# One PSUM bank per purpose, evictions queued at once, and dense work cut into quanta, in a fused encoder block

## The chip, the cores and the metric

The kernel runs on all 8 cores of one Trainium2 chip. Each core takes half of one sequence of the batch of four; there is no exchange between cores. The metric is device time in microseconds (us) of the slowest core. Most runs of one kernel agree within 0.3%, but some fall into a slow state; only fast runs are compared.

## The reference, cut to what matters

One encoder layer: normalization, one wide input projection, latent attention with 16 heads, a gated width-3 convolution, a merge of both, an output projection, and a last gated embedding.

```python
h   = rmsnorm(x);  z = h @ w_in                    # latents, rope key, gates, conv B/C/x, merge gates
q, kv from the latents (w_uq, w_ukv), per-head QK-norm, rope, softmax over 2048 keys
y_attn = (attn * silu(gate_a)) @ w_branch_attn
y_conv = (B * conv3(C * xin) * silu(gate_c)) @ w_branch_conv
x = x + (sigmoid(m_a) * y_attn + sigmoid(m_c) * y_conv) @ w_out
x = x + sigmoid(rmsnorm(x) @ w_ple_gate) * (p @ w_ple_proj)
```

Per core there are 1024 queries and 2048 keys. Three kinds of TensorE work meet in the middle of the kernel: the attention itself (16 heads x 16 steps of 128 keys), the small "pieces" that prepare the next head (Q, K, V from the latents, sums of squares) and close the last one, and "dense" groups of 16 matmuls each, for the attention gates (32 groups) and the eight channel blocks of the convolution (10 groups each).

## The kernel before: the parts that matter

PSUM, which all matmuls of the kernel write (`ps<-` in the traces), is used as eight banks. Scores take four (two steps in flight), the output two. Banks 6 and 7, `F`, are left for pieces and dense groups. Whoever needs a bank takes the one that is free and least recently used; the eviction (the operations that read the bank) is put on a list and queued later.

```python
F = [banks[6], banks[7]]
def grab(keep=False):                       # a bank for a piece, or (keep) for a dense group
    free = [i for i in (0, 1) if held[i] is None]
    i = min(free, key=lambda j: lastuse[j])
    ...
    flush()                                 # queues the evictions put off so far
    if keep: held[i] = True
    return i, F[i]

def proj16(tile_, rhs, n):                  # a dense group
    i, bk = grab(keep=True)
    for kc in range(16):
        mm(bk.ap[:, 0:n], tv[:, kc, :], rhs(kc), kc == 0, kc == 15, ...)
        yield n / 512.0                     # fill(n) asks for n of these at a time
    release(i)
    return bk

def qrope(i):                               # one of the pieces
    _, bk = grab()
    ...                                     # eight matmuls
    def ev(): ...                           # ACT square and VectorE product out of the bank
    deferred.append(ev)

for h in range(NH):                         # the attention; g = 16 * h + kt
    ...
    for kt in range(16):
        emit_S(g + 1)                       # scores of the next step into PSUM
        emit_exp(g + 1)                     # ACT: exp of them, 128x1024
        flush()                             # only now the evictions of the step before
        for fn in now:                      # pieces of the next head
            fn(); fill(budget / (len(now) + 1))
        fill(budget / (len(now) + 1))       # dense matmuls: gates and convolutions, some 5 a step
        emit_PV(g)
        emit_acc(g)                         # VectorE: running sum of the exponentials
```

ACT and VectorE work through their queues in order, as two pieces of trace below show: under run 4, ACT's copy of K starts at 612.01 us, behind an exp (611.00) before which ACT had been idle for 2.83 us; under run 7, VectorE's t1b starts at 669.78, behind Qn (668.27, after 0.33 us of waiting for ACT) and Qr (669.06). Semaphores are derived from the buffers that each operation reads and writes: a matmul that overwrites a bank waits for the operations that read it (here, in the attention, 41.8 us in 28 waits for fq alone).

Of the kernel before, what the change touches and what calls it, by code (L numbers as in the profile page):

```python
# [18 lines left out]
NH = 16  # L19
# [154 lines left out]
def build_nc():  # L174
# [20 lines left out]
    with ExitStack() as es:  # L195
# [61 lines left out]
        def mm(bank_ap, lhsT, rhs, start, stop, reads, writes, skip=False):  # L257
            if skip:
                return P.op("pe", lambda h: h.matmul(bank_ap, lhsT=lhsT, rhs=rhs, start=start, stop=stop, skip_group_check=True), reads=reads, writes=writes)  # L259
            return P.op("pe", lambda h: h.matmul(bank_ap, lhsT=lhsT, rhs=rhs, start=start, stop=stop), reads=reads, writes=writes)  # L260
# [141 lines left out]
        order = [("g", m) for m in range(6)]  # L402
        for it in ("c0 g6 c1 g7 c2 g8 c3 g9 g10 c4 g11 g12 c5 g13 c6 g14 c7 g15").split():
            order.append((it[0], int(it[1:])))
        for k_, i in order:
            if k_ == "g":
                ring.src.append((wt_d[i], 2048))
            else:
                for g_ in (0, 1, 2, 3):
                    ring.src.append((wt_d[16 + i * 4 + g_], 2048))  # L410
# [61 lines left out]
        def kv_tail(tb, b0, b1, bp, own):  # L472
# [20 lines left out]
            act(f_.ap, f_.ap, AF.Exp, [f_], [f_], scale=-0.5)  # L493
            for m, bm in enumerate((b0, b1)):
                stt(kvaT[m].ap[:, tsl], bm.ap, col(C_GKV + m), f_.ap, MUL, MUL, [bm, cols, f_], [kvaT[m]])
            _, bk = grab()
            mm(bk.ap, dupm.ap, kv_.ap, True, True, [dupm, kv_], [bk])
            P.op("act", lambda h, bk=bk: h.copy(out=KrT.ap[:, tsl], in_=bk.ap), reads=[bk], writes=[KrT])
            _, bk = grab()
            for j in range(4):  # L500
                mm(bk.ap[:, j:j + 1], sqpe.ap[0:64, j * 128:(j + 1) * 128], onesf.ap[0:64, 0:1], j == 0, j == 3, [sqpe, onesf], [bk], skip=True)
            vcopy(sspe.ap[:, tb * 4:(tb + 1) * 4], bk.ap[:, 0:4], [bk], [sspe])

# [22 lines left out]
        def proj16(tile_, rhs, n):  # L526
            i, bk = grab(keep=True)
            tv = tile_.ap.rearrange("p (c n) -> p c n", c=16)
            for kc in range(16):
                mm(bk.ap[:, 0:n], tv[:, kc, :], rhs(kc), kc == 0, kc == 15, [tile_, hT[kc]], [bk])  # L530
                yield n / 512.0
            release(i)
            return bk

        def gate_unit(m):
            tile_ = ring.take()
            for qb in range(2):
                sl = slice(qb * 512, (qb + 1) * 512)
                bk = yield from proj16(tile_, lambda kc: hT[kc].ap[:, sl], 512)
                e_ = eb[eb_i[0] % 2]  # L540
                eb_i[0] += 1

                def ev(bk=bk, e_=e_, sl=sl):
                    vcopy(zb.ap, bk.ap, [bk], [zb])
                    sigmoid_parts(e_, zb)
                    tt(AT[m].ap[:, sl], zb.ap, e_.ap, MUL, [zb, e_], [AT[m]])
                deferred.append(ev)
            ring.give(tile_)

        def conv_unit(c):  # L550
            tC, tX = ring.take(), ring.take()
            for i in range(3):
                sl = slice(i * 342, (i + 1) * 342)
                cc = ccb[i % 2]
                bk = yield from proj16(tC, lambda kc: hT[kc].ap[:, sl], 342)
                deferred.append(lambda bk=bk, cc=cc: P.op("act", lambda h: h.copy(out=cc.ap[:, 0:342], in_=bk.ap[:, 0:342]), reads=[bk], writes=[cc]))
                if i == 2:
                    ring.give(tC)
                bk = yield from proj16(tX, lambda kc: hT[kc].ap[:, sl], 342)

                def ev(bk=bk, cc=cc, i=i):
                    if i < 2:
                        tt(ub.ap[:, 1 + i * 342:1 + (i + 1) * 342], bk.ap[:, 0:342], cc.ap[:, 0:342], MUL, [bk, cc], [ub])
                    else:
                        tt(ub.ap[:, 685:1025], bk.ap[:, 0:340], cc.ap[:, 0:340], MUL, [bk, cc], [ub])
                        tt(ub.ap[:, 0:1026:1025], bk.ap[:, 340:342], cc.ap[:, 340:342], MUL, [bk, cc], [ub])
                deferred.append(ev)
            ring.give(tX)
            tG, tB = ring.take(), ring.take()
            for qb in range(2):  # L570
                sl = slice(qb * 512, (qb + 1) * 512)
                bk = yield from proj16(tG, lambda kc: hT[kc].ap[:, sl], 512)
                e_ = eb[eb_i[0] % 2]
                eb_i[0] += 1

                def evg(bk=bk, e_=e_, qb=qb):
                    o = qb * 512
                    vcopy(zb.ap, bk.ap, [bk], [zb])
                    sigmoid_parts(e_, zb)
                    ts(yb.ap, ub.ap[:, o:o + 512], col(C_CW + 3 * c), col(C_CB_ + c), MUL, ADD, [ub, cols], [yb])  # L580
                    stt(yb.ap, ub.ap[:, o + 1:o + 513], col(C_CW + 3 * c + 1), yb.ap, MUL, ADD, [ub, cols, yb], [yb])
                    stt(yb.ap, ub.ap[:, o + 2:o + 514], col(C_CW + 3 * c + 2), yb.ap, MUL, ADD, [ub, cols, yb], [yb])
                    tt(e_.ap, zb.ap, e_.ap, MUL, [zb, e_], [e_])
                deferred.append(evg)
                if qb == 1:
                    ring.give(tG)
                bk = yield from proj16(tB, lambda kc: hT[kc].ap[:, sl], 512)

                def evb(bk=bk, e_=e_, sl=sl):
                    tt(t1b.ap, bk.ap, yb.ap, MUL, [bk, yb], [t1b])  # L590
                    tt(cvg[c].ap[:, sl], t1b.ap, e_.ap, MUL, [t1b, e_], [cvg[c]])
                deferred.append(evb)
            ring.give(tB)

        def dense():
            for k_, i in order:
                yield from (gate_unit(i) if k_ == "g" else conv_unit(i))

        dgen = dense()
        dleft = [16.0 * 32 + 8 * 128]  # L600

        def fill(n):
            while n > 0:
                c_ = next(dgen, None)
# [3 lines left out]
                dleft[0] -= c_  # L608

        for kc in range(16):  # L610
# [13 lines left out]
            flush()  # L624
            fill(6)
# [3 lines left out]
        for qb in range(2):  # L629
# [5 lines left out]
            act(rstr.ap[:, sl], rstr.ap[:, sl], AF.Exp, [rstr], [rstr], scale=-0.5)  # L635
        for tb in range(2, 4):
# [36 lines left out]
        def up_pieces(h):  # L673
# [8 lines left out]
            def qnope(qb):  # L682
                sl = slice(qb * 512, (qb + 1) * 512)
                _, bk = grab()
                for kc in range(4):
                    mm(bk.ap, wn[:, kc, :], qaT[kc].ap[:, sl], kc == 0, kc == 3, [w, qaT[kc]], [bk])

                def ev():
                    vcopy(q0[qb].ap, bk.ap, [bk], [q0[qb]])
                    act(qsq[qb].ap, q0[qb].ap, AF.Square, [q0[qb]], [qsq[qb]])  # L690
                deferred.append(ev)

            def qrope(i):
                _, bk = grab()
                for kc in range(4):
                    for qb in range(2):
                        mm(bk.ap[qb * 64:qb * 64 + 64, :], wr[:, kc, i * 64:i * 64 + 64], qaT[kc].ap[:, qb * 512:(qb + 1) * 512], kc == 0, kc == 3, [w, qaT[kc]], [bk])

                def ev():
                    if i == 0:  # L700
                        act(qsq[2].ap, bk.ap, AF.Square, [bk], [qsq[2]])
                        stt(t12[0].ap, bk.ap, col(C_GQR), cosQ.ap, MUL, MUL, [bk, cols, cosQ], [t12[0]])
                    else:
                        stt(t12[1].ap, bk.ap, colx.ap[:, 0:1], sinQ.ap, MUL, MUL, [bk, colx, sinQ], [t12[1]])
                        tt(t12[0].ap, t12[0].ap, t12[1].ap, ADD, [t12[0], t12[1]], [t12[0]])
                deferred.append(ev)

            def qss(qb):
                sl = slice(qb * 512, (qb + 1) * 512)
                r = slice(qb * 64, qb * 64 + 64)  # L710
                _, bk = grab()
                mm(bk.ap, ones.ap, qsq[qb].ap, True, False, [ones, qsq[qb]], [bk])
                mm(bk.ap, ones.ap[r, :], qsq[2].ap[r, :], False, True, [ones, qsq[2]], [bk])

                def ev():
                    act(fq[qb].ap, bk.ap, AF.Ln, [bk, cols], [fq[qb]], bias=col(C_EPS), scale=1.0 / 192)
                    act(fq[qb].ap, fq[qb].ap, AF.Exp, [fq[qb]], [fq[qb]], scale=-0.5)
                    stt(Q_.ap[:, sl], q0[qb].ap, colx.ap[:, 2:3], fq[qb].ap, MUL, MUL, [q0[qb], colx, fq[qb]], [Q_])
                    tt(R_.ap[r, :], t12[0].ap[r, :], fq[qb].ap[r, :], MUL, [t12[0], fq[qb]], [R_])
                deferred.append(ev)  # L720

            def kup(tb):
                sl = slice(tb * 512, (tb + 1) * 512)
                _, bk = grab()
                for kc in range(2):
                    mm(bk.ap, wk[:, kc, :], kvaT[kc].ap[:, sl], kc == 0, kc == 1, [w, kvaT[kc]], [bk])

                def ev():
                    vcopy(K_.ap[:, sl], bk.ap, [bk], [K_])
                    act(ksq[tb].ap, K_.ap[:, sl], AF.Square, [K_], [ksq[tb]])  # L730
                deferred.append(ev)

            def kss():
                _, bk = grab()
                for j in range(16):
                    s_ = ksq[j // 4]
                    mm(bk.ap[:, j:j + 1], s_.ap[:, (j % 4) * 128:(j % 4 + 1) * 128], ones.ap[:, 0:1], j == 0, j == 15, [s_, ones], [bk], skip=True)

                def ev():
                    tt(skt[p].ap, bk.ap[:, 0:16], sspe.ap, ADD, [bk, sspe], [skt[p]])  # L740
                    act(skt[p].ap, skt[p].ap, AF.Ln, [skt[p], cols], [skt[p]], bias=col(C_EPS), scale=1.0 / 192)
# [331 lines left out]
```

## Time and profile before

Before: 2084.93 us, median of 4 runs (2082.27 to 2136.24).

| stretch of the profiled run (span 2081 us) | length, us | what it does |
|---|---|---|
| 0 to 133 | 133 | own half of x, latents, own keys |
| 133 to 265 | 132 | other half of x, latents' tail, first head's pieces; 171 of 512 gate matmuls |
| 265 to 1445 | 1180 | attention with pieces and dense work |
| 1445 to 2081 | 636 | merge, output projections |

The first part of the page gives busy time of each engine with its share of the span and the number of instructions:

```profile
PE 1719.6 (83%) x8022; PEld 719.4 (35%) x8022; DVE 899.9 (43%) x1104; ACT 728.8 (35%) x974; POOL 88.4 (4%) x171
```

No engine is near full over the whole. A share of busy time is an average of stages with different limits, so the reading has to go stage by stage, as the prediction does. (In the tables of the trace PE is TensorE, PEld its weight loads, DVE VectorE, ACT ScalarE, SP the queue that issues transfers.)

### The profile page before, as it was taken

What the parts mean: (1) busy time and instruction counts of PE and PEld (TensorE: products, weight loads), DVE (VectorE), ACT (ScalarE), POOL (GpSimd) and SP (SyncE); (2) the same over time, 40 slices, a digit from 0 to 9 for tenths busy, and PEclk for the clock granted to TensorE, in tenths of its full rate; (3) what the DMA queues carried; (4) which work ended last, traced back from release to release, by engine and by line L of the source; (5) the groups of instructions that cost most, each with busy time, mean ns of one, the idle gap of its engine ahead of it and who ended that gap; (6) DMA issues with size and microseconds to landing.
All of it is one profiled execution on the core that took longest, in us unless ns stands there. A gap on an engine that the chain in (4) does not pass through costs nothing.

```text
span 2081.2 us, 22355 instructions; the slowest of 8 cores (2069.4 to 2081.2 us)
## 1 busy us (share of the span) xinstructions
PE 1719.6 (83%) x8022; PEld 719.4 (35%) x8022; DVE 899.9 (43%) x1104; ACT 728.8 (35%) x974; POOL 88.4 (4%) x171
## 2 busy tenths in 40 slices
PE   3686777778777778777778877779999999999998
PEld 1232223333322323232333322323444444444444
DVE  3723444545544455444445555446111111134455
ACT  3546344444433444444444444445100100111211
POOL 0000000000000000000000000000100000010000
PEclk8898788999988889898898998889999999999999
DMA  9513012112111112111111012011644555588462
GB/s 215 148 61 81 11 29 28 21 18 39 29 21 28 18 21 38 19 20 28 28 21 28 14 29 36 6 21 26 96 71 71 75 81 82 82 172 179 85 141 76
DMA packets 36428, 119.53 MB, mean 57 GB/s; under 512 B 4192, under 2 KB 4320, under 8 KB 35936
## 3 DMA queue, kind: packets, MB, share of 16 engines
q0 software_dynamic: 24048, 82.85, 26.2%
q1 hardware_dynamic: 12272, 35.26, 5.2%
q8 instruction: 66, 1.08, 0.2%
q14 instruction: 42, 0.34, 0.1%
HBM read 192.01 MB, written 8.39 MB: 96 GB/s over the span
## 4 chain that ended last, share of the span: by engine, by line
PE 70%; ACT 11%; DVE 9%; issue 7%; DMA 2%; ACTq 0%; SPq 0%; DVEq 0%; POOL 0%; POOLq 0%
PE ps L260 68%; ACT P L263 3%; ACT eb L263 2%; DVE acc L274 2%; DMA xo<-x_own 2%; PE ps L259 2%; ACT acc L263 1%; ACT fq L263 1%; DVE Kn L277 1%; ACT ksq L263 1%; DVE zb L277 1%; DVE t L266 1%; ACT V L754 1%; DVE Osb L274 1%; ACT qsq L263 1%
## 5 line engine op out<-in xcount | busy, mean ns | idle before, releaser
L260 PE MATMUL ps<-hT,ring 128*128 128x512 bf16 (+1 forms) x2432 | 595.2, 385 | 84.8 <-DVE Kn L277 31.4
L263 ACT ACTIVATE P<-ps,sk 128x1024 bf16<-128x1024 f32 x256 | 284.6, 1113 | 530.2 <-PE ps L260 483.2
L260 PEld LDWEIGHTS ps<-hT,ring 128*128 128x128 bf16 x2432 | 234.8, 103 | 387.8 <-issue 211.0
L274 DVE TENSOR_TENSOR acc<-acc,P 128x1024 f32<-128x1024 f32 x224 | 273.4, 1220 | 15.7 <-ACT P L263 5.0
L266 DVE SCALAR_TENSOR_TENSOR mt<-mt,ps 128x512 f32<-128x512 f32 x64 | 44.0, 687 | 312.8 <-PE ps L260 312.8
L260 PE MATMUL ps<-P,V 128*128 128x512 bf16 x512 | 172.7, 422 | 0.1
L260 PE MATMUL ps<-Qn,Kn 128*128 128x512 bf16 x512 | 169.9, 417 | 0.0
L263 ACT ACTIVATE mt<-ps 128x512 f32<-128x512 f32 x64 | 38.2, 597 | 339.8 <-PE ps L260 339.8
L260 PE MATMUL ps<-qaT,wup 128*64 128x512 bf16 (+1 forms) x384 | 75.1, 418 | 58.0 <-DVE t L266 25.9
L255 POOL DMA_DIRECT2D ring<-w_tiles x95 | 50.1, 528 | 1687.9 <-PE ps L260 1685.3
L260 PE MATMUL ps<-Qr,KrT 64*128 64x512 bf16 x512 | 105.0, 407 | 0.0
L260 PE MATMUL ps<-hT,ringm 128*128 128x512 bf16 x384 | 85.5, 379 | 0.0
L260 PEld LDWEIGHTS ps<-Qn,Kn 128*128 128x128 bf16 x512 | 54.4, 106 | 74.5 <-issue 24.6
L260 PEld LDWEIGHTS ps<-P,V 128*128 128x128 bf16 x512 | 54.6, 107 | 58.4 <-issue 17.5
L260 PE MATMUL ps<-AT,ring 128*128 128x512 bf16 x320 | 72.3, 379 | 0.0
L274 DVE TENSOR_TENSOR Osb<-Osb,acc 128x1024 f32<-128x1024 f32 x16 | 19.6, 1225 | 117.9 <-ACT acc L263 117.9
L260 PE MATMUL ps<-acc,onesf 128*128 128x512 f32 x68 | 42.1, 706 | 34.2 <-ACT acc L263 27.7
L260 PE MATMUL ps<-kvaT,wup 128*128 128x512 bf16 x128 | 43.0, 421 | 33.0 <-ACT fq L263 21.9
L277 DVE CAST Kn<-ps 128x512 bf16<-128x512 f32 x64 | 44.0, 688 | 60.4 <-ACT ksq L263 42.0
L266 DVE SCALAR_TENSOR_TENSOR Qn<-q,colx,fq 128x512 bf16<-128x512 f32 x32 | 24.0, 751 | 100.9 <-ACT fq L263 100.9
L260 PEld LDWEIGHTS ps<-Qr,KrT 64*128 64x128 bf16 x512 | 24.8, 93 | 123.8 <-issue 123.8
L260 PE MATMUL ps<-xg,wlq 128*128 128x512 bf16 x128 | 36.8, 451 | 37.1 <-ACT xg L263 36.6
(138 smaller groups left out, 1858.1 us busy)
## 6 DMA issues: line engine op xcount, KB each, us to landing
ring<-w_tiles POOLq DMA_DIRECT2D x95, 512.0 KB, 6.2
ringm<-w_tiles POOLq DMA_DIRECT2D x33, 512.0 KB, 7.3
xo<-x_own SPq DMA_DIRECT2D x16, 513.0 KB, 31.9
xr<-x_rest SPq DMA_DIRECT2D x16, 512.0 KB, 4.4
x<-x_own SPq DMA_DIRECT2D x16, 512.0 KB, 41.4
out<-x SPq DMA_DIRECT2D x32, 256.0 KB, 3.3
wup<-w_up POOLq DMA_DIRECT2D x16, 384.0 KB, 8.5
ring<-w_bc POOLq DMA_DIRECT2D x10, 256.0 KB, 6.4
```

What stands on the lines that cost most here:

```text
L255: return P.dma(eng, lambda h: h.dma_start(out=o_ap, in_=in_ap), slot, reads=reads, writes=[b], deps=deps)
L259: return P.op("pe", lambda h: h.matmul(bank_ap, lhsT=lhsT, rhs=rhs, start=start, stop=stop, skip_group_check=True), reads=reads, writes=wr ...
L260: return P.op("pe", lambda h: h.matmul(bank_ap, lhsT=lhsT, rhs=rhs, start=start, stop=stop), reads=reads, writes=writes)
L263: return P.op("act", lambda h: h.activation(out=out, in_=in_, func=func, **kw), reads=reads, writes=writes)
L266: return P.op("dve", lambda h: h.scalar_tensor_tensor(out=out, in0=in0, scalar=scalar, in1=in1, op0=op0, op1=op1), reads=reads, writes=writes)
L274: return P.op("dve", lambda h: h.tensor_tensor(out=out, in0=in0, in1=in1, op=op), reads=reads, writes=writes)
L277: return P.op("dve", lambda h: h.tensor_copy(out=out, in_=in_), reads=reads, writes=writes)
L754: P.op("act", lambda h: h.copy(out=V_.ap[:, r * 512:(r + 1) * 512], in_=bk.ap), reads=[bk], writes=[V_])
```

## The change

Its intent: TensorE should never wait for a bank in the attention. Pieces get bank 7 and nothing else. Dense groups get bank 6 and are cut into quanta of four to six matmuls, of which a step takes one; the generator of dense work stops where a group ends, so that a group never starts in the step in which another ended. Evictions are queued right after their matmuls. All gate groups go ahead of the attention, into gaps of the stretch before it, and their activation becomes one tanh where it was exp, ln, exp; the factor 2 is taken up in the softmax sum's logarithm. K is copied by ACT and squared by VectorE, where it was the other way round. Three smaller moves come along: the running sum is queued ahead of the pieces, a head's output is multiplied by its gate straight out of PSUM, and the next head's weights are fetched earlier. The diff, cut to its core:

```diff
-            _, bk = grab()
-            ...
-            def ev(): ...
-            deferred.append(ev)
+        def qrope(i, bk):                    # and so all pieces: the bank is given, the
+            ...                              # eviction follows the matmuls at once
+        def group(tile_, rhs, n, cuts, give=False):
+            bk = banks[6]
+            for kc in range(16):
+                mm(bk.ap[:, 0:n], tv[:, kc, :], rhs(kc), kc == 0, kc == 15, ...)
+                if kc + 1 in cuts:
+                    yield False              # a quantum ends inside the group
+        CUT3, CUT4 = (5, 10), (4, 8, 12)
+        ...                                  # conv_unit: "yield True" after each group's eviction
+        def quantum():
+            at_cut[0] = next(cgen, True)
+        bU, bD = banks[7], banks[6]
+        ...                                  # all 512 gate matmuls, and the first head's pieces
                 if g + 1 < NG:
                     emit_S(g + 1)
                     emit_exp(g + 1)
-                flush()
-                ...
-                for fn in now:
-                    fn()
-                    fill(budget / (len(now) + 1))
-                fill(budget / (len(now) + 1))
+                emit_acc(g)
+                if pieces:
+                    pieces.pop(0)(bU)
+                if at_cut[0] and len(pieces) >= 16 - kt:
+                    pieces.pop(0)(bD)        # the 17th piece of a head
+                else:
+                    quantum()
                 emit_PV(g)
-                emit_acc(g)
```

## The prediction

> **What bounds the kernel now.** I read the granted clocks of all cores first (0.917 to 0.926, spans 2069 to 2081 us: one state, no odd core), then the page's slices:
>
> ```profile
> PE   3686777778777778777778877779999999999998
> PEclk8898788999988889898898998889999999999999
> ```
>
> A slice is 52 us. From slice 6 to 28, the attention heads, TensorE is busy some 7 tenths at an unsteady clock; behind that it is full at full clock. Busy time by stage (columns: stretch, its length, then busy us with counts for PE, PEld, DVE, ACT, POOL, then clock, DMA share, GB/s):
>
> ```profile
> 133.00:222.00 89.00, 63.82 (x224) 26.94 (x224) 34.74 (x41) 50.51 (x63) 1.58 (x3) 0.84 0.32 83
> 222.00:265.00 43.00, 31.68 (x161) 12.06 (x161) 17.30 (x27) 17.95 (x30) 1.58 (x3) 0.89 0.16 24
> 265.00:1445.00 1180.00, 917.68 (x4479) 365.18 (x4479) 594.84 (x709) 520.27 (x691) 29.52 (x56) 0.89 0.16 24
> 1445.00:2081.00 636.00, 627.26 (x2887) 283.03 (x2885) 189.63 (x263) 86.56 (x127) 50.13 (x95) 1.00 0.56 100
> ```
>
> No engine is full in the attention's 1180 us: TensorE stands 262 us, DVE and ACT more, DMA is at 0.16. So it is bound by waits. TensorE's waits there:
>
> ```profile
> PE ps L260 <- ACT fq L263: 41.8, 28, 2.1
> PE ps L260 <- ACT acc L263: 41.1, 23, 2.7
> PE ps L260 <- DVE Kn L277: 40.6, 25, 2.5
> PE ps L260 <- DVE t L266: 39.6, 19, 3.1
> ```
>
> All are waits of a matmul for the eviction of a PSUM bank, about 2 us each. Two pieces of the timeline show a stalled and a smooth step:
>
> ```profile
> 832.29 0.59 PE L260 MATMUL ps<-Qn,Kn 128*128 128x512 bf16 x2
> 832.82 0.39 PE L260 MATMUL ps<-Qr,KrT 64*128 64x512 bf16 x2
> 835.94 1.92 PE L260 MATMUL ps<-qaT,wup 128*64 128x512 bf16 x8 [2.73 <-DVE t L266]
> 837.79 2.20 PE L260 MATMUL ps<-hT,ring 128*128 128x512 bf16 x6
> ...
> 1413.34 1.04 PE L260 MATMUL ps<-hT,ring 128*128 128x512 bf16 x4
> 1414.22 0.59 PE L260 MATMUL ps<-P,V 128*128 128x512 bf16 x2
> 1414.65 0.59 PE L260 MATMUL ps<-Qn,Kn 128*128 128x512 bf16 x2
> 1415.17 0.39 PE L260 MATMUL ps<-Qr,KrT 64*128 64x512 bf16 x2
> 1415.50 1.04 PE L260 MATMUL ps<-hT,ring 128*128 128x512 bf16 x4
> ```
>
> The first waits 2.73 us and then does its next matmuls at half speed (8 in 1.85 us; the same 8 took 0.98 us at 829.57). The second, with no small pieces to evict, makes a step of ten matmuls in 2.155 us: 0.2155 us each, no gap.
>
> Why the wait is so long: two banks (6, 7) serve both the small pieces that prepare the next head and the dense projections. A dense group holds its bank over several steps, so consecutive pieces share the other one, and their evictions are deferred until the next step's exp (1.11 us) has been queued on ACT. A piece's bank comes free only after S, exp, ACT work and often a DVE operation of the next step.
>
> [...] So a removed wait is worth more than itself. [...] 636 us of dense work on all eight cores ran at 1.00. [...] The trace has 5 loads of 1283 ns[...].
>
> **The change, part by part.** TensorE's instructions are the same in number; they move.
>
> *a. One bank per purpose, no deferral.* Pieces always use bank 7, one per step (a 17th goes into bank 6 where the dense work is at a cut); dense groups use bank 6, cut into quanta of 4 to 6 matmuls, one per step. Each eviction is queued at once. An eviction now has from the piece to the next step's piece: quantum, PV and S, some 2 us.
>
> *b. What the attention holds.* Per step S and PV: 2.155 - 4 x 0.2155 = 1.29 us; 256 steps 331 us. Pieces of one head, at full clock from the timeline: qnope 2 x 0.88, qrope 2 x 0.98, kup 4 x 0.44, qss 2 x 0.63, kss 0.40, vup 4 x 0.46: 9.0 us, 15 heads 135. Sums of the tail, 0.96 each, 30 of them: 29. Dense before: 853 matmuls of 512 columns (184) and 768 of 342 at 0.147 (113): 297. Sum before 792; so 1180 - 792 = 388 us are loss, 262 standing and 126 slow clock. That checks: 0.11 of clock missing x 1180 = 130.
> After, the gates go out: the convolutions' 272 quanta hold 223 us, of which 15 quanta (12 us) are done ahead and 15 (13 us) are left for the end, so 198. Sum after: 331 + 135 + 29 + 198 = 693 us, 2.71 per step.
>
> *c. The other engines per step after.* ACT per head: exp 16 x 1.11, pieces about 11, convolution 2.4: 31 us, 1.95 per step. DVE: acc 15 x 1.22, pieces 12, convolution 5: 36 us, 2.2 per step. Moves between them (64 K copies from DVE to ACT, 64 squares back, gates with one tanh for three ACT operations, Osb scaled straight out of PSUM, one 1.2 us DVE operation less per head) are small. Both stay below 2.71, DVE at 82%.
>
> *d. Before the attention.* The 512 gate matmuls (110 us) move here, where 171 dense were done. The loop over the other half's x: 14 matmuls per turn, 3.02 us against ACT's 1.98, 16 turns 48 us (before 65: ACT had the sigmoids in it). The latent's tail: chain of 25 us before, some 22 with fills in its waits and a steady clock. Then 32 + 104 + 80 gate matmuls 46.5 us, the first head's pieces with 120 more and 15 quanta 47, table loads and the first exp 4. From 134: attention begins at about 301 instead of 265, so +36.
>
> *e. After it.* 15 quanta, 13 us with 2 of waits on the single bank, against 4 now: +11. The rest stays at some 632.
>
> *f. Stalls left over.* DVE and ACT run in order. At each of 16 gate groups of a convolution 2.7 us of DVE and 1.9 us of ACT come at once and delay the next evictions past the next piece: about 0.8 us each, 13. 15 times qrope's ACT-then-DVE eviction misses its 2 us by 0.3: 4. The other group ends, qss pieces blocking DVE at a group's end, head changes: 18. Sum 35.
>
> Total: 301 + 693 + 35 + 15 + 632 = 1676 span, about 1680 as time.
>
> **Rivals.** *DVE becomes the bound.* For: 82% share and bursts, queues in order. Against: 36 us per head against TensorE's 43. It would make the attention some 100 us longer: 1780. *The standing returns under another name*, the eviction being longer than its 2 us in most steps: 0.5 us per step are 128 us and some of the half clock, 1830. Against it: an exp ends 2.2 us after the step's start, a 0.6 us eviction at 2.9, and the next piece is due at 3.5. *The work only moves*: 341 gate matmuls (73 us) leave the attention and are paid ahead; if the waits stayed, the gain would be nearly none. Against: waits come from pieces, and their buffering is what changes. [...] *Ring loads late* in the gate stretch: a tile each 6.9 us from four slots, landing in 6.2, as in the end stage now; hardly.
>
> **Range and chances.** The floor with no stall at all is 1640. The likely fault is to have too few stalls; twice the 35 us is 1715, and the first rival in part some 1740. So 1680, range 1645 to 1745; faster 0.97, same 0.02, slower 0.01.
>
> **What would show it.** The attention should last 720 to 740 us with a clock of 0.97 or more and TensorE above 90% busy; the four waits above shrunk from 163 to under 40 us in all; the first P at about 300; the gates' stretch full of TensorE. Wrong would be: a clock that stays at 0.9; waits of TensorE on bank 7's evictions of 0.5 us in every step; DVE near full in the attention; a first P after 320.

What is cut, as marked, are statements about the clock, PSUM's banks and the loads of ACT's function table that no trace or run here shows, and a rival built on one of them (a denser attention held at a lower clock, +160 us). That a removed wait is worth more than itself rests on what is quoted above it: the same eight matmuls took 1.85 us after a wait of 2.73 us, and 0.98 at 829.57. The 5 loads of 1283 ns are those of ACT's function table in the kernel before. The 4 us for "table loads and the first exp" in *d* are an estimate whose numbers aren't given; by the trace before, two loads of 1.28 us and an exp of 1.11 make 3.7.

## The result, and the profile after

The changed kernel took 1717.01 us, median of 10 runs (1715.87 to 1962.71; two runs of these were slow ones, at 1868.90 and 1962.71). Before, over the same rounds and those ahead of them: 2085.17 us (15 runs). The ratio is 0.8243 (95% interval 0.8224 to 0.8262): faster. Ratios here are the mean time of one kernel's fast runs over that of the other's fast runs of the same rounds, so they are not quite the ratio of the medians quoted. The result is correct against the reference, as it is for every kernel below.

The busy times, the slices of TensorE and its clock (a slice is now 43 us), from the page after:

```profile
PE 1586.0 (92%) x8022; PEld 697.0 (41%) x8022; DVE 857.3 (50%) x1084; ACT 684.6 (40%) x902; POOL 89.0 (5%) x171
PE   2689999899899899989989999999999999999998
PEclk8889999999999999999999999999999999999999
```

The same 8022 matmul instructions are busy for 134 us less: nothing was taken away from TensorE, it runs near full clock now (0.981 on this core, 0.919 before). The 7 tenths of the attention have become 9. By stage (columns as in the prediction):

```profile
0.00:136.00 136.00, 80.14 (x274) 32.23 (x274) 64.15 (x67) 54.15 (x64) 5.62 (x14) 0.85 0.56 139
136.00:184.60 48.60, 48.34 (x224) 22.09 (x225) 22.82 (x24) 31.51 (x32) 2.11 (x4) 1.00 0.66 160
184.60:207.00 22.40, 18.77 (x74) 8.16 (x72) 10.43 (x16) 10.69 (x17) 1.05 (x2) 1.00 0.19 31
207.00:255.20 48.20, 48.20 (x226) 22.00 (x226) 17.29 (x27) 14.11 (x25) 3.69 (x7) 1.00 0.41 74
255.20:309.00 53.80, 48.70 (x285) 24.29 (x283) 15.70 (x27) 22.11 (x32) 2.63 (x6) 0.97 0.23 40
309.00:1066.00 757.00, 702.77 (x3996) 299.46 (x3997) 532.34 (x654) 464.00 (x605) 22.70 (x44) 0.99 0.17 29
```

The attention went from 1180 to 757 us, its clock from 0.89 to 0.99; the stretch ahead of it from 132 to 173 us, with three times the gate matmuls in it (512 for 171). What is behind the attention is 649 us long, 13 more than before, with the last 15 quanta of the convolution in it. 423 - 41 - 13 = 369 us, against 366 between the two spans (the stretch up to 133 or 136 us makes the rest).

TensorE's waits in the attention of the changed kernel (us in total, times, longest):

```profile
PE ps L260 <- ACT acc L263: 13.3, 6, 3.2
PE ps L260 <- ACT Kn L738: 7.0, 5, 1.4
PE ps L260 <- DVE ub L274: 6.5, 7, 1.9
PE ps L260 <- DVE zb L277: 6.2, 4, 2.0
PE ps L260 <- DVE q L277: 5.5, 8, 0.9
...
PE ps L260 <- ACT fq L263: 0.7, 1, 0.7
PE ps L260 <- DVE t L266: 0.5, 2, 0.3
```

All waits together are 55 us, where they were 262. The four that led the list before (163 us) make 21.5. A step of the steady kind in the changed kernel:

```profile
614.88 0.59 PE L260 MATMUL ps<-P,V 128*128 128x512 bf16 x2
615.31 0.59 PE L260 MATMUL ps<-Qn,Kn 128*128 128x512 bf16 x2
615.83 0.39 PE L260 MATMUL ps<-Qr,KrT 64*128 64x512 bf16 x2
616.15 0.71 PE L260 MATMUL ps<-qsq,ones 128*128 128x512 bf16 x2
616.80 0.90 PE L260 MATMUL ps<-hT,ring 128*128 128x342 bf16 x5
617.54 0.59 PE L260 MATMUL ps<-P,V 128*128 128x512 bf16 x2
```

One piece (qsq), one quantum (five matmuls of 342 columns), and no bracket, that is no wait, in 2.66 us.

### The profile page after: what moved, and what is told of

Its sections match the earlier page's. It is cut to its first block, busy times and chain, and to the rows that moved or that the text cites. A ratio compares the mean times of both kernels' runs of the same rounds, so it can differ in the third digit from the quotient of the medians.

```text
span 1715.0 us, 22381 instructions; the slowest of 8 cores (1706.9 to 1715.0 us)
## 1 busy us (share of the span) xinstructions
PE 1586.0 (92%) x8022; PEld 697.0 (41%) x8022; DVE 857.3 (50%) x1084; ACT 684.6 (40%) x902; POOL 89.0 (5%) x171
## 4 chain that ended last, share of the span: by engine, by line
PE 83%; ACT 5%; DVE 4%; issue 4%; DMA 2%; SPq 0%; ACTq 0%; DVEq 0%
PE ps L260 81%; PE ps L259 3%; DMA xo<-x_own 2%; ACT P L263 1%; ACT acc L263 1%; DVE acc L274 1%; ACT fq L263 1%; DVE zb L277 0%; DVE q L277 0%; DVE Qr L274 0%; ACT L263 0%; ACT eb L263 0%; DVE Qn L266 0%; DVE ub L274 0%; SPq L255 0%
## 5 line engine op out<-in xcount | busy, mean ns | idle before, releaser
L260 PE MATMUL ps<-hT,ring 128*128 128x512 bf16 (+1 forms) x2432 | 524.9, 358 | 30.9 <-DVE ub L274 9.9
L263 ACT ACTIVATE P<-ps,sk 128x1024 bf16<-128x1024 f32 x256 | 284.2, 1111 | 212.2 <-PE ps L260 185.1
L260 PEld LDWEIGHTS ps<-hT,ring 128*128 128x128 bf16 x2432 | 226.4, 98 | 281.8 <-issue 78.5
L274 DVE TENSOR_TENSOR acc<-acc,P 128x1024 f32<-128x1024 f32 x224 | 273.2, 1220 | 28.6 <-ACT P L263 26.9
L263 ACT ACTIVATE mt<-ps 128x512 f32<-128x512 f32 x64 | 38.2, 597 | 338.1 <-PE ps L260 338.1
L260 PE MATMUL ps<-Qn,Kn 128*128 128x512 bf16 x512 | 153.8, 382 | 1.8 <-DVE AT L266 1.8
L260 PE MATMUL ps<-P,V 128*128 128x512 bf16 x512 | 154.0, 383 | 0.0
L260 PE MATMUL ps<-Qr,KrT 64*128 64x512 bf16 x512 | 100.3, 389 | 0.0
L260 PE MATMUL ps<-hT,ringm 128*128 128x512 bf16 x384 | 85.5, 379 | 0.0
L260 PEld LDWEIGHTS ps<-Qn,Kn 128*128 128x128 bf16 x512 | 50.2, 98 | 63.9 <-issue 4.7
L260 PE MATMUL ps<-xg,wlq 128*128 128x512 bf16 x128 | 37.7, 457 | 38.6 <-ACT xg L263 38.3
L260 PE MATMUL ps<-AT,ring 128*128 128x512 bf16 x320 | 72.3, 379 | 0.0
L260 PE MATMUL ps<-qaT,wup 128*64 128x512 bf16 (+1 forms) x384 | 67.2, 386 | 5.4 <-DVE q L277 4.4
L260 PEld LDWEIGHTS ps<-Qr,KrT 64*128 64x128 bf16 x512 | 24.6, 93 | 109.9 <-issue 109.9
L260 PEld LDWEIGHTS ps<-P,V 128*128 128x128 bf16 x512 | 49.9, 98 | 47.0 <-issue 7.4
L260 PE MATMUL ps<-xg,ring 128*128 128x512 bf16 x288 | 65.1, 379 | 0.0
L263 ACT ACTIVATE tp<-tp 128x512 f32<-128x512 f32 x32 | 20.1, 630 | 95.8 <-DVE tp L274 95.8
L263 ACT ACTIVATE sq<-x 128x1024 f32<-128x1024 f32 x16 | 16.9, 1057 | 100.1 <-DVE x L266 100.1
L260 PEld LDWEIGHTS ps<-hT,ringm 128*128 128x128 bf16 x384 | 37.6, 98 | 45.2
L260 PE MATMUL ps<-merged,ringm 128*128 128x512 bf16 x256 | 55.7, 379 | 0.0
```

Of the source, the lines that this page charges most:

```text
L260: return P.op("pe", lambda h: h.matmul(bank_ap, lhsT=lhsT, rhs=rhs, start=start, stop=stop), reads=reads, writes=writes)
L263: return P.op("act", lambda h: h.activation(out=out, in_=in_, func=func, **kw), reads=reads, writes=writes)
L274: return P.op("dve", lambda h: h.tensor_tensor(out=out, in0=in0, in1=in1, op=op), reads=reads, writes=writes)
```

## The experiments

Twelve runs (the fifth is the changed kernel again) were made, each beside the kernel before. Standing is the sum of TensorE's waits in the attention, read from each trace from the first to the last step; the clock is the mean in that stretch.

| run | fast time, us | ratio to before | attention, us | standing, us | clock |
|---|---|---|---|---|---|
| before | 2085 | 1 | 1180 | 262 | 0.89 |
| changed kernel | 1717 | 0.8243 | 757 | 55 | 0.99 |
| 1 before, evictions not deferred | 1879 | 0.899 | 967 | 133 | 0.96 |
| 2 before, own banks, deferred (flawed) | 2115 | 1.0117 | 916, no dense work in it | 284 | 0.82 |
| 3 before, own banks, not deferred (flawed) | 1889 | 0.9059 | 684, no dense work in it | 140 | 0.93 |
| 4 changed, evictions deferred | 2245 | 1.074 | 1287 | 372 | 0.79 |
| 5 changed, again | 1717 | 0.8235 | 757 | 53 | 0.99 |
| 6 changed, halves of the sums apart | 1704 | 0.8175 | 745 | 44 | 0.99 |
| 7 changed, VectorE's order | 1692 | 0.8115 | 732 | 36 | 0.99 |
| 8 both | 1679 | 0.8052 | 719 | 26 | 1.00 |
| 9 changed, gates inside | 1734 | 0.8314 | 843 | 61 | 0.99 |
| 10 changed, K's copies back | 1729 | 0.8293 | 769 | 65 | 0.99 |
| 11 changed, not cut at groups' ends | 1845 | 0.8839 | 896 | 141 | 0.94 |
| 12 before, own banks, not deferred | 1953 | 0.937 | 1041 | 196 | 0.95 |

The theory: TensorE waited because an eviction came late (deferral), because pieces and dense groups shared two banks, and, with own banks, because a group would follow another at once; the gates' removal only moves work. The rivals: deferral is everything (A); the gates leaving the attention is the gain (B); separate banks are everything (C).

**1. Before, without deferral.**

```diff
-        deferred = []
+        class Now(list):
+            def append(self, fn):
+                fn()
+        deferred = Now()
```

> The kernel before, with one edit: an eviction is queued as soon as its matmuls are, not after the next step's exp. Banks and work stay. My theory (both the deferral and the shared pair of banks make the waits): about half the gain, 1800 to 1930 us, TensorE's standing in the attention falling from 262 us to 100-150. Rival A (deferral is the whole cause): 1750 or less. Rival B (what counts is that the gates leave the attention): over 2040.

1879.3 us median, 0.899 (0.8949 to 0.903); standing 133 us. Half of the gain, from the order of the queues alone: no instruction less, no bank more. Rival A falls, since 162 us to the changed kernel are left; so does B in its strict form, since the gates stayed inside.

**2 and 3. Before, with own banks, with and without deferral: not what was meant.** The edit gave a piece bank 7 and a group bank 6 from the attention on. To change over it ran dense matmuls until no group was open. But a group that ends is followed by the next in the same call, so this never came true until all dense work was done: it ran ahead of the attention (from 265 to some 565 us), which held only pieces.

```diff
-            i = min(free, key=lambda j: lastuse[j])
+            i = (0 if keep else 1) if own_bank[0] else min(free, key=lambda j: lastuse[j])
 ...
+        while held[0] or held[1]:
+            fill(1)
+        own_bank[0] = True
         NG = NH * 16
```

> The kernel before with bank 7 for pieces and bank 6 for dense groups in the attention; evictions still deferred. My theory: no gain or a loss, 2030 to 2250 us, since every step's piece now waits for an eviction queued behind the exp just before it, and dense groups follow each other on one bank. Rival C (separate banks are the cause of the gain): 1850 or less.

> The kernel before with both edits: own banks and no deferral; gates still in the attention, groups not cut at the end of a step. My theory: pieces hardly wait, but each of some 85 dense groups of the attention starts on the bank that the last one has just filled and waits about 1.5 us: 1830 to 1950 us. If the cutting into quanta is worth nothing: 1740 or less. If moving the gates is the gain: over 2000.

Run 2: 1.0117 (1.0047 to 1.0187), run 3: 0.9059 (0.8974 to 0.9144). The times lie inside what I had written, for another reason than the one written, so they don't count for the theory as worded. They still answer two questions. First, taking all dense work out of the attention does not give the gain: run 2 is no faster than the kernel before, which rival B can't explain. Second, the two differ in the deferral alone, with the same work in the attention (columns: stretch, length, busy us of PE, PEld, DVE, ACT, POOL, clock, DMA share, GB/s; the first line is of run 2, the second of run 3):

```profile
562.00:1478.00 916.00, 630.45 (x2854) 214.47 (x2853) 480.67 (x524) 439.52 (x558) 7.95 (x15) 0.82 0.04 7
```

```profile
568.00:1252.00 684.00, 543.49 (x2853) 196.76 (x2853) 474.12 (x522) 441.36 (x559) 7.24 (x14) 0.93 0.06 10
```

The deferral costs 232 us here, and the same matmuls are busy for 87 us longer, at a clock of 0.82 and not 0.93.

**4. The changed kernel, with deferral again.** Everything but TensorE's instructions that a piece or a quantum issues is held back and queued after the next step's exp.

```diff
                     emit_exp(g + 1)
+                P.flush_held()
                 emit_acc(g)
+                P.hold = True
                 ...                       # piece, quantum
+                P.hold = False
                 emit_PV(g)
```

> The changed kernel with the evictions of the attention's pieces and groups deferred again until the next step's exp is queued. My theory: nearly every one of some 240 steps with a piece stands about 1.5-2 us for bank 7 and the clock falls under 0.93: 2050 to 2350 us, at or above the kernel before. If the deferral is harmless where each purpose has its own bank: 1715 to 1760.

2244.5 us median, 1.074 (1.0698 to 1.0782): slower than the kernel before, as expected. One step of its trace, with the lines that matter (the helpers' line numbers are shifted by the edit: L271 and L274 here are L260 and L263 elsewhere):

```profile
610.42 0.39 PE L271 MATMUL ps<-Qr,KrT 64*128 64x512 bf16 x2
611.00 1.11 ACT L274 ACTIVATE P<-ps,sk 128x1024 bf16<-128x1024 f32 x1 [2.83 <-PE ps L271]
612.01 0.58 ACT L749 CAST Kn<-ps 128x512 bf16<-128x512 f32 x1
...
612.73 0.59 PE L271 MATMUL ps<-kvaT,wup 128*128 128x512 bf16 x2 [1.92 <-ACT Kn L749]
...
613.16 1.35 PE L271 MATMUL ps<-hT,ring 128*128 128x342 bf16 x6
```

Scores, then the exp of 1.11 us, then the copy of K out of bank 7, and only then TensorE's next piece: 1.92 us of wait. ACT itself had been idle for 2.83 us before the exp, so the copy, of a piece of the step before, could have been made then; it stood in the queue behind an exp whose scores weren't there yet. And the six matmuls after it take 1.14 us to the next instruction where they take 0.88 at full clock (614.00 to 614.88 in the step of the changed kernel).

**9. The changed kernel with gates in the attention.** 320 of 512 gate matmuls go back in as quanta on bank 6, with the old three activations.

```diff
+        def gate_q(m):
+            tile_ = ring.take()
+            for qb in range(2):
+                bk = yield from group(tile_, ..., 512, CUT4, qb == 1)
+                vcopy(zb.ap, bk.ap, [bk], [zb])
+                sigmoid_parts(e_, zb)
+                stt(AT[m].ap[:, sl], zb.ap, 2.0, e_.ap, MUL, MUL, [zb, e_], [AT[m]])
+                yield True
```

> The changed kernel's banks, quanta and immediate evictions, but 320 of the 512 gate matmuls go back into the attention, as quanta on bank 6 with the old three-activation sigmoid. My theory (moving the gates only moves work): the attention gets 69 us longer by their matmuls and the stretch before it shorter by the same; with more bursts on ACT and VectorE 1715 to 1755 us in all. Rival B (the gates leaving the attention is the gain): 1850 or more.

1734.0 us, 0.8314 (0.8298 to 0.8331), so 17 us over the changed kernel's 1717.

```profile
184.60:259.00 74.40, 54.85 (x298) 26.77 (x299) 32.39 (x54) 29.51 (x50) 2.64 (x5) 0.91 0.22 37
259.30:1102.40 843.10, 781.66 (x4337) 333.18 (x4336) 562.18 (x702) 500.49 (x668) 27.96 (x53) 0.99 0.19 32
```

The attention is 86 us longer (69 us of gates, and, by the prediction's count, some 13 us of the 15 quanta that the changed kernel leaves for the end), it starts 50 us earlier, and what follows it is 17 us shorter. TensorE stays 93% busy in it. So the gates' matmuls cost about the same inside; what their removal brings is that they fill gaps ahead of the attention, where TensorE is busy for only 55 of 74 us here. The 17 us hold the old three activations too. Rival B is refuted.

**11. The changed kernel, with cuts that miss the groups' ends.**

```diff
-        CUT3, CUT4 = (5, 10), (4, 8, 12)
+        CUT3, CUT4 = (3, 8, 13), (2, 6, 10, 14)
 ...                                       # and no "yield True" after a group
```

> The changed kernel, with the cuts between quanta moved into the groups, so that no step ends where a dense group ends: the last matmuls of one group and the first of the next lie in one step, on the same bank. Immediate evictions and own banks stay (the 17th piece of a head moves to the head's end). My theory (the first three experiments leave open what the cutting is worth): some 71 boundaries wait 1.2 to 1.8 us each for the eviction just queued, 85 to 130 us, and the 17th pieces 10 to 30: 1800 to 1880 us, most of TensorE's standing in front of dense matmuls. Rival (own banks and no deferral are enough): 1745 or less.

1845.4 us, 0.8839 (0.8794 to 0.8884). Its waits:

```profile
PE ps L260 <- DVE ub L274: 44.5, 22, 4.0
PE ps L260 <- DVE zb L277: 31.7, 16, 3.7
PE ps L260 <- ACT ccb L582: 31.7, 22, 2.4
PE ps L260 <- DVE t1b L274: 27.2, 15, 3.7
PE ps L260 <- DVE V L277: 3.9, 14, 0.5
```

ub, ccb, zb and t1b are the four ways in which a dense group leaves bank 6. 75 waits make 135 us, 1.8 each; the 17th pieces cost under 4 us, less than I had allowed. Same banks, same matmuls, evictions at once: 128 us hang on where the work is cut.

**12. Before, with own banks and no deferral, as meant.** The group that is open at the change keeps its bank, and pieces take the other.

```diff
-            i = min(free, key=lambda j: lastuse[j])
+            i = (own_bank[0] if keep else 1 - own_bank[0]) if own_bank else min(free, key=lambda j: lastuse[j])
 ...
+        own_bank.append(1 if held[1] else 0)
```

> The third experiment as it was meant: the kernel before with no deferral and, from the first step of the attention on, one bank for pieces and one for dense groups, and this time the dense work stays in the attention. My theory: pieces hardly wait, the dense groups do, at each boundary: 1820 to 1900 us, little different from no deferral alone (1879), with the standing moved from pieces to dense matmuls. If own banks are worth much by themselves: 1780 or less.

1953.1 us, 0.937 (0.9353 to 0.9386): above my range, and 74 us slower than run 1, which shares the banks. The group of dense matmuls in its attention, with the idle time before them and what ended it:

```profile
L260 PE MATMUL ps<-hT,ring 128*128 128x512 bf16 (+1 forms) x1613 | 371.4, 357 | 169.1 <-DVE zb L277 60.6 <-DVE ub L274 44.1 <-ACT ccb L561 35.9
L260 PE MATMUL ps<-qaT,wup 128*64 128x512 bf16 (+1 forms) x354 | 65.4, 396 | 4.0 <-DMA wup<-w_up 2.3 <-DVE q L277 0.9 <-issue 0.5
```

The pieces hardly wait any more, the dense groups wait 169 us, where they wait 66 in run 1. I had the place of the waits right and their number and length too small: 97 waits of 1.7 us. Own banks without the cut are a loss; with the cut, and the rest of the change, they make run 9's 1734. Rival C falls. These 219 us are more than the cut's 128 in run 11, and the rest is known only in part: the gate groups inside add waits (zb 60.6 us in 35 waits here, 31.7 in 16 in run 11), K's copies were 12 us in run 10, and the smaller moves were not run alone.

**5, 6, 7 and 8. What was left in the changed kernel.** In 6, the two halves of the softmax sum are tracked as two buffers: the second half's matmul had waited for the Ln and Exp that write the first. In 7, VectorE's order is changed: the convolution's operations at a gate group's end are spread over three steps, and operations that need a result of ACT are queued one step later.

```diff
-                mm(bk.ap, onesf.ap, a.ap[:, sl], True, True, [onesf, a], [bk])
+                mm(bk.ap, onesf.ap, a.ap[:, sl], True, True, [onesf, ah[qb]], [bk])    # run 6
 ...
+                late.append(lambda: (stt(Q_...), tt(R_...)))       # run 7, queued after the next acc
+                bk = yield from group(tB, ..., qb == 1, conv_ops)  # one of them at each cut
```

> The changed kernel again, as the yardstick of this call: 1712 to 1722 us.

> The changed kernel, with the two halves of the softmax sums tracked as two buffers, so that the second half's matmul no longer waits for the first half's Ln and Exp. My theory (13 us of TensorE's 54 us standing in the attention are this wait): 8 to 13 us faster than the yardstick, 1704 to 1709 us. If that standing is absorbed elsewhere: within 3 us.

> The changed kernel, with VectorE's order changed: the convolution's four operations at a gate group's end are spread over the next three steps, and operations that wait for ACT (scaling of Q, squares of K) are queued one step later, so that they do not block the in-order queue. My theory (bursts and blocking on VectorE make about 30 of the 54 us): 15 to 30 us faster than the yardstick, 1687 to 1702 us. If ACT's own queue is what holds the banks: within 6 us.

> Both mends together. My theory: they add up, 25 to 40 us faster than the yardstick, 1677 to 1692 us, with under 20 us of standing left in the attention.

Medians 1716.5, 1704.4, 1691.8 and 1678.7 us; the ratios' intervals (0.822 to 0.8249, 0.8161 to 0.819, 0.8101 to 0.8129, 0.8038 to 0.8066) lie apart. So 12 and 25 us, and 38 together, where the sum of the two is 37: they add up. The traces agree: TensorE's wait for acc (ACT), 13.3 us in the changed kernel, is gone in run 6, and its waits for ub, zb and t1b fall from 17.2 to 2.1 us in run 7. What 7 mends can be seen in the changed kernel:

```profile
667.47 0.63 ACT L263 ACTIVATE fq<-fq 128x512 f32<-128x512 f32 x1
...
668.27 0.75 DVE L266 SCALAR_TENSOR_TENSOR Qn<-q,colx,fq 128x512 bf16<-128x512 f32 x1 [0.33 <-ACT fq L263]
...
669.06 0.69 DVE L274 TENSOR_TENSOR Qr<-t,fq 64x512 bf16<-64x512 f32 x1
...
669.78 0.69 DVE L274 TENSOR_TENSOR t1b<-ps,yb 128x512 f32<-128x512 f32 x1
...
670.62 1.36 PE L260 MATMUL ps<-hT,ring 128*128 128x512 bf16 x4 [1.77 <-DVE t1b L274]
...
671.77 1.06 PE L260 MATMUL ps<-P,V 128*128 128x512 bf16 x2
```

The group's eviction (t1b) is ready to go (the group's last matmul started at 666.74), but stands in VectorE's queue behind Qn, which waits for ACT, and Qr, which nobody needs soon. In run 8 the attention reads:

```profile
309.30:1028.30 719.00, 693.22 (x3992) 297.98 (x3992) 528.54 (x654) 462.00 (x605) 22.25 (x42) 1.00 0.18 30
```

26 us of standing are left, a little over the 20 that I expected. Run 8 is the best version, 2.2% ahead of the changed kernel (0.8052 / 0.8235).

**10. K copied by VectorE and squared by ACT again.**

```diff
-                P.op("act", lambda h: h.copy(out=K_.ap[:, sl], in_=bk.ap), reads=[bk], writes=[K_])
-                tt(ksq[tb].ap, K_.ap[:, sl], K_.ap[:, sl], MUL, [K_], [ksq[tb]])
+                vcopy(K_.ap[:, sl], bk.ap, [bk], [K_])
+                act(ksq[tb].ap, K_.ap[:, sl], AF.Square, [K_], [ksq[tb]])
```

> The changed kernel with the 64 copies of K back on VectorE and the 64 squares back on ACT, as before. My theory (a small move): VectorE gets 0.27 us more each, its bursts reach the K pieces' bank: 3 to 15 us slower than the changed kernel, 1720 to 1732 us. If the move was important: over 1750.

1728.9 us, 0.8293 (0.8278 to 0.8307), so 12 us. (The 0.27 us written for VectorE are the 688 ns of a copy of K in the kernel before less the 424 ns of a square in the changed one.) TensorE's wait for K is 19.9 us in 17 waits, where it was 7.0: the same copy comes later when it stands in the busier queue (VectorE is busy for 547 of 769 us, ACT for 472; that the queue is the reason is argued).

## Why the prediction was right

The time was 1680 us and the range 1645 to 1745; measured were 1717. By its parts:

- *What binds, and the 388 us of loss.* Right. The count of pure matmul time in the changed attention, 693 us, was met by run 8: 693.2 us busy at a clock of 1.00, in an attention of 719. ("About 2 us each" was a little high: the four waits it lists average 1.7.)
- *a, one bank, no deferral.* Right in mechanism, and runs 1, 4, 9, 11 and 12 show its parts: deferral alone is worth 206 us from the side of before (2085 to 1879) and 528 from the side of after (2245 to 1717); own banks are a loss of 74 us without the cut (run 12 against 1), and the cut is worth 128 us with them (run 11). The prediction named the cut as part of the design, and gave it no number.
- *b, the gates go out.* Right: their 69 us inside are paid ahead, and the net worth, with the single activation, is 17 us (run 9).
- *c, no engine becomes the bound.* Right: VectorE is busy for 532 of 757 us, ACT for 464. The counts were some 7% high (36 and 31 us per head make 576 and 496), on the safe side. Of the "small moves" only K's copies were run alone, at 12 us; for the output scaled out of PSUM and the place of the sum, small is not shown.
- *d, the start of the attention.* 301 predicted, 309.4 measured. The loop over x (48.6 us), the latent's tail (22.4) and the gates' stretch (48.2) were met within 2 us; the first head's pieces with table loads took 53.8 for 51, and the opening stretch 2 us longer. The trace has six loads of ACT's function table between 272 and 298 us, one at each change between the gates' tanh and the pieces' Ln. A change took 1.30 us here (275.45 to the next activation at 276.75). TensorE waits 1.92 us (at 278.78) and 1.77 us (at 299.90) for evictions in this stretch; that the loads cause those waits is argued, not tested.
- *e, after the attention.* 649 for 647.
- *f, stalls left over.* This term was mis-sized, as the prediction thought likely (twice the 35 us would be 1715, it wrote): 35 us written, 55 of standing measured and some 10 of slow clock (703 us busy for a count of 693). Missing in it was the false dependency between the halves of the sum (12 us by run 6), and VectorE's blocking was put too low: the waits at gate groups were listed with 13 us and blocking within 18, the order of VectorE gave 25 (run 7). The attention is 757 - 728 = 29 us over, its start 8, the end 2: together the 39 us between the spans (1715 measured, 1676 worked out).
- *What would show it.* Clock 0.99, TensorE 93% busy, the four waits at 21.5 us: as written. The attention's 757 us missed the written 720 to 740, and the first P came at 310.5 for "about 300".
- *Rivals.* VectorE as the bound, standing in most steps, and late loads did not come. A lower clock did, but only in the two slow runs: one die's clocks were 0.819 to 0.832 in the one of 1962.71 us and 0.882 to 0.894 in the one of 1868.90. What set them isn't shown.

## What to carry to other kernels

When no engine is full, list what ended TensorE's waits: if they are evictions of about the same length, look at where the eviction stands in its engine's queue before looking for more banks or faster operations. Give each stream of work its own bank, queue evictions at once but behind nothing that waits itself, and cut the work so that a bank's next user comes a full step after its last; of these the order and the cut were worth more than the banks. Then count the pure matmul time at full clock: what is over it is waits and the slow clock behind them (262 us and, by the prediction's count, 126 in the kernel before). The two mends of runs 6 and 7 took 38 us of it away together (run 8), each by the waits that it was aimed at.

## What the traces show of the clock and of VectorE

- *The clock after a wait.* Here waits of some 2 us can be followed by half-rate matmuls: after 1.77 us in the changed kernel (at 670.62 us) come two matmuls in 1.06 us instead of 0.59, and in run 4, where 30 waits for fq make 63.0 us (the longest 3.8) and 45 for Kn 87.3 (the longest 2.4), the mean clock of the attention was 0.79. The length of one wait doesn't decide it here: after 1.76 us in the kernel before (at 829.57 us) the next eight matmuls took 0.98 us, full rate. What does decide it isn't shown.
- *The clock under dense work.* Read core by core, all eight ran the 636 us at the end of the kernel before at 0.99 to 1.00, and all cores of the changed kernel had 0.980 to 0.987 over the whole profiled run. A clock of 0.819 to 0.832 on one die shows in one of the two slow runs among eleven of the changed kernel; the other had 0.882 to 0.894.
- *VectorE and 16-bit tensors.* At this kernel's 512 elements, a product of 16-bit tensors (ksq, changed kernel) takes 424 ns and one of 32-bit tensors (AT<-zb,eb before, written as 16 bit) 692, a factor of 1.6.
